# Hybrid encoder layer: `w_proj_b` as two block products of seven multiplications whose products take turns, with the b gates by way of DRAM and weight sums made in DRAM

## The chip, the cores and the metric

The kernel runs on one core of a Trainium2 chip. A core has five engines that each work through their own queue in order: TensorE (PE) multiplies matrices into PSUM, VectorE (DVE) and ScalarE (ACT) do elementwise work, GpSimd (POOL) does elementwise work in SBUF and issues DMAs, SyncE (SP) issues DMAs. Engines wait for each other through semaphores. The metric is the device time of one execution in microseconds. Everything is float32. A product of two matrices is made of three TensorE matmuls on float32r operands: each operand is split into a high part (`hi`, a cast) and a low part (`lo`, source minus high), and high x high, high x low and low x high are added up.

## The reference

One layer for 512 tokens of width 1024. What bears on the change is the mixer: one input projection feeds an S5 branch, a gated spatial branch and two gates, and the two branches are merged.

```python
n = rms_norm(h, mix_norm_g[i])
proj = n @ w_in[i]
xa = proj[..., :OFF_U]
zu = proj[..., OFF_U:OFF_V]
zv = proj[..., OFF_V:OFF_GA]
gate_a = jax.nn.sigmoid(proj[..., OFF_GA:OFF_GB])
gate_b = jax.nn.sigmoid(proj[..., OFF_GB:])
ya = s5_branch(xa, ...)
yb = sgu_branch(zu, zv, sgu_ln_g[i], sgu_ln_b[i], sgu_w[i], sgu_bias[i])
merged = gate_a * (ya @ w_proj_a[i]) + gate_b * (yb @ w_proj_b[i])
h = h + merged @ w_out[i]
h = h + memory_cross_attention(rms_norm(h, xattn_norm_g[i]), memn, w_q[i], w_k[i], w_v[i], w_xo[i])
h = h + swiglu(rms_norm(h, ffn_norm_g[i]), w_gate[i], w_up[i], w_down[i])
```

`yb` is 512 x 1024, `w_proj_b` 1024 x 1024. The S5 branch is two state-space scans over the sequence, a GELU and a gated projection (`w_glu`).

## The kernel before

**Weights.** All weights stream from DRAM by a plan: a list of entries, each with the loads to issue and the split to make. `next_w` (line 286) takes the next entry; it starts loads three entries ahead (`LOADS`), and makes high and low parts two entries ahead (`SPLITS`). Raw weights, high parts and low parts have three buffers each. Loads go through SP's queue.

**Two ways of multiplying.** `feat` (line 316) takes 256 output columns over all 512 tokens: a block of four 128-row tiles is 24 matmuls of 512 columns. `product` (line 1255) is one of the products of a two-by-two block multiplication in the Strassen-Winograd form: 24 matmuls of 256 columns. There a pair of 512 weight columns needs seven products instead of eight, with sums of quarters of the operands made beforehand. The feed-forward stage works so; `w_down`'s weight sums are made in DRAM by copies (`dsum`, SP) and accumulating copies (POOL), spread over the plan by `plan_sums` (line 216).

**The stages around the change.** After `zu` (the spatial branch, which yields `yb_hi`, `yb_lo` in slots E and D) a loop takes 256 columns at a time: gate b (`w_in`, 2 blocks of weights), whose sigmoid goes into `part` in slot A, then `w_proj_b` (2 blocks), whose result is multiplied into `part` (line 989). Four turns of the loop are 8 gate blocks and 8 `w_proj_b` blocks.

**S5 beside it.** S5 is a generator (`s5_program`) that `tick` advances between blocks. The scan over 64 chunks is 62 steps of four small VectorE instructions. Then come four octets of groups. For each octet `s5_outputs` (line 807) copies the shifted states `ss` (ScalarE, four copies) and multiplies into `py` on TensorE with `tt` (L822), `e` and `ss` (L823, L824); `emit` applies GELU and stores `y` to DRAM (`yd`) by eight small DMAs. `tt` holds the octet's kernels: made on TensorE (`pk`), stored to DRAM (`kd`) and loaded back by eight POOL DMAs (L743) into one buffer. Octets 2 and 3 have their `pk` between the outputs of the octets before. When all is drained (`finish_side`), `ygt` is loaded from `yd` (L1005) into memory that S5 has freed, split into `yg_hi` and `yg_lo`, and `w_glu` is multiplied.

**What sets the order.** The program is written in one order, and a scheduler with a model of times moves instructions of an engine against each other when the kernel is built. On the chip each engine then keeps that order.

Of the kernel before, what the change touches and what calls it, by code (L numbers as in the profile page):

```python
# [9 lines left out]
F32 = mybir.dt.float32  # L10
F32R = mybir.dt.float32r
# [6 lines left out]
P = 128  # L18
# [21 lines left out]
Q = 8  # L40
# [12 lines left out]
def hybrid_layer_kernel(  # L53
# [146 lines left out]

    DOWN, CHUNKS = (1, 5, 2, 6, 3, 7, 4), 6
    DSRC = {1: (0, 0), 2: (1, 0), 3: (1, 1)}
    dsum = {q: dp.tile([P, NF // 2, 512], F32, name=f"dsum{q}") for q in (4, 5, 6, 7)}
# [8 lines left out]
    def plan_sums(first, step):  # L216


        more = {5: lambda c: down_block(0, 1, c), 7: lambda c: down_block(1, 1, c),
                6: lambda c: down_sum(5, c), 4: lambda c: down_sum(6, c)}  # L220

        def start(q, i, jc, c):
            tc.keep_in_program_order(nc.sync.dma_start(down_sum(q, c), down_block(i, jc, c)))

        def add(q, c):
            nc.gpsimd.dma_start(down_sum(q, c), more[q](c), accum_op=ALU.add)

        j = first
        for q, i, jc in ((5, 0, 0), (7, 0, 1), (6, 1, 1), (4, 1, 0)):
            for c in range(CHUNKS):  # L230
                plan[j][1].append((0, lambda x=(q, i, jc, c): start(*x)))
                plan[j + step][1].append((0, lambda x=(q, c): add(*x)))
                j += step

    def plan_down(w, make_tokens, entries):
        for q in DOWN:
            for c in range(CHUNKS):
                got = {}

                def load(q=q, c=c, got=got):  # L240
                    src = down_block(*DSRC[q], c) if q in DSRC else down_sum(q, c)
# [10 lines left out]
    for c0 in range(0, SW, 256):  # L252
        plan_feat(w_in, c0, KD)
    plan_tok(w_in, OFF_V + 512, KD)
    first_copy = len(plan)
# [222 lines left out]
    def slot(tag, shape, dt, name):  # L478
        return sp.tile(list(shape), dt, tag=tag, name=name)

    def token_slot(name, shift=0):
# [44 lines left out]
    def s5_setup():  # L526
# [23 lines left out]
        for nm, src in (("br", s5_b_re), ("bi", s5_b_im), ("cr", s5_c_re), ("ci", s5_c_im)):  # L550
            if nm[0] == "b":
                row = s5p.tile([G, 2, 64, C], F32, tag="u", name="row" + nm)
                nc.sync.dma_start(row, src[0].rearrange("d g p c -> g d p c"))
                rows = row.rearrange("g d p c -> g (d p) c")
            else:
                row = s5p.tile([G, C, 2, 64], F32, tag="u", name="row" + nm)
                for d in range(2):
                    nc.sync.dma_start(row[:, :, d, :], src[0, d])
                rows = row.rearrange("g c d p -> g (d p) c")
            ps = aux("pbc", (P, C, G))  # L560
            for c in range(C):
                nc.tensor.transpose(ps[:, c, :], rows[:, :, c], ident[:G, :G])
            t = s5p.tile([P, G, C], F32, name="raw_" + nm)
            A_.copy(t, ps.rearrange("p c g -> p g c"))
            bc.append(t)
            yield 0.1
# [42 lines left out]
        st["pe"], st["pw"] = [], []  # L609
        for src in (pr, pi):  # L610
            pe = s5p.tile([P, G, Q], F32, name="pe%d" % len(st["pe"]))
            pw = s5p.tile([P, G, Q], F32, name="pw%d" % len(st["pw"]))
# [355 lines left out]
    yb_hi = slot("E", (P, KD, T), F32R, "yb_hi")  # L968
    yb_lo = slot("D", (P, KD, T), F32R, "yb_lo")
    yb = (yb_hi, yb_lo)  # L970

    def zu_evac(m, j, ps):
        h = m - OFF_U // P
# [6 lines left out]
        feat(w_in, c0, xn, KD, zu_evac)  # L980


    part = slot("A", (P, KD, T), F32, "part")

    def gb_evac(m, j, ps):
        nc.scalar.activation(part[:, m - OFF_GB // P, :], ps, AF.Sigmoid)

    def pb_evac(m, j, ps):
        nc.vector.tensor_tensor(part[:, m, :], ps, part[:, m, :], ALU.mult)

    for c0 in range(0, D, 256):
        feat(w_in, OFF_GB + c0, xn, KD, gb_evac)
        feat(w_proj_b, c0, yb, KD, pb_evac)
    finish_side()
    s5.close()
    mgx = ExitStack()
# [231 lines left out]
        nc.vector.tensor_tensor(pair[:, j, :], pair[:, j, :], ps, ALU.mult)  # L1228


    K0, K1, T0, T1 = slice(0, 4), slice(4, 8), slice(0, 256), slice(256, 512)
    a11, a12, a21, a22 = full[:, K0, T0], full[:, K1, T0], full[:, K0, T1], full[:, K1, T1]

    def make_op(q, i, src):
# [15 lines left out]
        make_op(3, 4, a12)  # L1250

    fn_q = lambda ks, ts: (fn_hi[:, ks, ts], fn_lo[:, ks, ts])
    ops = {1: fn_q(K0, T0), 2: fn_q(K1, T0), 7: fn_q(K0, T1), 4: fn_q(K1, T1)}

    def product(ps, u, q, start):

        hi, lo = next_w(u[0], u[1], q)
        for j in range(2):
            cs = slice(j * P, (j + 1) * P)
            for k in range(4):  # L1260
                a = (hi[:, k, cs], lo[:, k, cs])
                b = (ops[q][0][:, k, :], ops[q][1][:, k, :])
                for i, (x, y) in enumerate(((0, 0), (0, 1), (1, 0))):
                    nc.tensor.matmul(ps[:, j, :], a[x], b[y], start=start and j == k == i == 0,  # L1264
                                     stop=k == 3 and i == 2, skip_group_check=True)
        tick(2.7)

    def unit_bank(name):
        return bank(name).rearrange("p (j t) -> p j t", j=2)

    def unit_start(u):
        x, v = unit_bank("px"), unit_bank("pv")
# [84 lines left out]
    for i, u in enumerate(UNITS):  # L1357
# [7 lines left out]
        if i == 0:  # L1365
            split(*fn_q(K0, T1), s3)
        product(x, u, 6, False)
        u2 = stp[0].tile([P, 2, 256], F32, tag="u2", name="u2", bufs=2)
        u3 = np_.tile([P, 2, 256], F32, tag="ev", name="u3", bufs=2)
        nc.scalar.copy(u2, x)  # L1370
        if not final:
# [150 lines left out]
```

## Time and profile before

| what | value |
|---|---|
| three timed runs | 914.30, 914.52, 915.68 us (median 914.52) |
| the profiled execution | 915.85 us, its span 914.1 us |
| VectorE, ScalarE busy | 609.0 us, 458.7 us |
| DMA | 142.77 MB, mean 156 GB/s |
| gate b and `w_proj_b`, with three and a half S5 octets | 220 to 338 us of the span |
| the feed-forward units | 612 to 805 us |

The span runs from the first to the last recorded instruction; the execution's time holds a little more around it. In the views, "PE" is a matmul and "PEld" a weight load, a name such as `pf<-xn,whi` says what is written and read, and "<-" in brackets names what ended a wait. The chain of waits is followed back from the last instruction.

### The profile page before, as it was taken

Reading aid. Unit: us, or ns where it says so; the run is one execution under the profiler, and the core shown is the slowest. Engines: PE = TensorE matmul, PEld = TensorE weight load, DVE = VectorE, ACT = ScalarE, POOL = GpSimd, SP = SyncE. Lnnn points to the kernel's source line nnn. Section 1 sums busy time; section 2 is a strip of 40 time slices with the busy share of each in tenths; the row PEclk is TensorE's granted clock in tenths of the full one; section 3 lists DMA queues with packets and bytes.
Section 4 is the critical chain, followed back from the end, with each engine's and each line's share of the span. In section 5 each row is a group of like instructions: output and inputs, shape, how many; then the busy total and the mean of one; then the engine's idle time right before and its main releaser. Section 6 shows DMA issues by size and latency. Waiting matters only on the chain.

```text
span 914.1 us, 14130 instructions
## 1 busy us (share of the span) xinstructions
PE 897.4 (98%) x5510; PEld 789.2 (86%) x5510; DVE 609.0 (67%) x991; ACT 458.7 (50%) x671; POOL 109.1 (12%) x163
## 2 busy tenths in 40 slices
PE   7999999999999999999999999999999999999996
PEld 6888888888888887789998888999999999888875
DVE  5596662888753235868545444786778777899875
ACT  5542995244374333445434433655554555655663
POOL 3003210000025301502000001000000000000000
PEclk8999999999999999999999999999999999999999
DMA  8445263675546655686895217415456463246572
GB/s 269 127 120 151 85 164 126 181 205 133 141 138 158 144 185 156 216 260 191 244 291 147 71 68 233 113 65 142 119 154 144 118 160 94 70 147 207 188 241 82
DMA packets 105987, 142.77 MB, mean 156 GB/s; under 512 B 13232, under 2 KB 73152, under 8 KB 105920
## 3 DMA queue, kind: packets, MB, share of 16 engines
q1 hardware_dynamic: 90688, 120.14, 40.9%
q0 software_dynamic: 12064, 19.37, 12.9%
q10 hardware_dynamic: 3168, 2.36, 0.9%
q8 instruction: 43, 0.70, 0.3%
q14 instruction: 24, 0.20, 0.1%
HBM read 135.06 MB, written 29.85 MB: 180 GB/s over the span
## 4 chain that ended last, share of the span: by engine, by line
PE 86%; ACT 4%; DVE 4%; DMA 3%; issue 2%; POOL 1%; POOLq 0%; SPq 0%; ACTq 0%; DVEq 0%
PE pf L314 31%; PE pt L314 14%; PE px L1264 12%; PE pq L1264 6%; PE dx L314 5%; PE dq L314 3%; PE pv L1264 3%; PE dv L314 2%; PE pk L714 2%; DVE wlo L86 1%; PE ptr L466 1%; PE po L314 1%; PE psc L314 1%; DMA wraw<-dsum 1%; ACT whi L85 1%
## 5 line engine op out<-in xcount | busy, mean ns | idle before, releaser
L86 DVE TENSOR_TENSOR wlo<-wraw,whi 128x1024 fp32r<-128x1024 f32 (+1 forms) x130 | 157.9, 1216 | 130.5 <-ACT whi L85 128.0
L85 ACT CAST whi<-wraw 128x1024 fp32r<-128x1024 f32 x132 | 135.4, 1028 | 174.5 <-PE pf L314 79.7
L314 PE MATMUL pf<-xn,whi 128*128 128x512 f32 x448 | 140.5, 392 | 0.0
L314 PEld LDWEIGHTS pf<-xn,whi 128*128 128x128 f32 x448 | 83.7, 188 | 17.3 <-issue 0.2
L314 PE MATMUL pf<-xn,wlo 128*128 128x512 f32 x224 | 87.6, 391 | 0.0
L1264 PE MATMUL px<-fn,whi 128*128 128x256 f32 x480 | 83.8, 277 | 0.0
L1264 PEld LDWEIGHTS px<-fn,whi 128*128 128x128 f32 x480 | 72.6, 188 | 0.3 <-ACT u L1377 0.2
L85 ACT CAST whi<-b 128x1024 fp32r<-128x1024 f32 x40 | 42.1, 1054 | 55.0 <-PE px L1264 26.8
L86 DVE TENSOR_TENSOR wlo<-b,whi 128x1024 fp32r<-128x1024 f32 x40 | 48.9, 1223 | 28.5 <-ACT whi L85 28.5
L1264 PE MATMUL px<-fn,wlo 128*128 128x256 f32 x240 | 66.3, 276 | 0.0
L314 PE MATMUL dx<-whi,s 128*128 128x512 f32 x170 | 53.9, 391 | 1.4 <-ACT whi L85 1.0
L1264 PE MATMUL pq<-s,whi 128*128 128x256 f32 x320 | 55.0, 276 | 0.0
L314 PEld LDWEIGHTS pf<-xn,wlo 128*128 128x128 f32 x224 | 42.1, 188 | 8.5
L1264 PEld LDWEIGHTS pq<-s,whi 128*128 128x128 f32 x320 | 48.3, 188 | 0.2
L86 DVE TENSOR_TENSOR wlo<-t,whi 128x1024 fp32r<-128x1024 f32 x30 | 36.7, 1224 | 15.9 <-ACT whi L85 15.9
L85 ACT CAST whi<-t 128x1024 fp32r<-128x1024 f32 x30 | 31.6, 1053 | 31.0 <-PE pv L1264 11.3
L314 PE MATMUL pt<-whi,xn 128*128 128x512 f32 x128 | 43.4, 412 | 1.8 <-ACT xn L85 1.5
L1264 PEld LDWEIGHTS px<-fn,wlo 128*128 128x128 f32 x240 | 45.1, 188 | 0.0
L1264 PE MATMUL pq<-s,wlo 128*128 128x256 f32 x160 | 44.2, 276 | 0.0
L314 PE MATMUL pf<-hn,whi 128*128 128x512 f32 (+1 forms) x160 | 41.8, 349 | 0.0
L314 PEld LDWEIGHTS dx<-whi,s 128*128 128x128 f32 x170 | 31.7, 188 | 8.5 <-ACT whi L85 1.2
L314 PE MATMUL dx<-wlo,s 128*128 128x512 f32 x85 | 33.3, 391 | 0.7 <-DVE wlo L86 0.7
(380 smaller groups left out, 2175.3 us busy)
## 6 DMA issues: line engine op xcount, KB each, us to landing
wraw<-in_w_in_dram SPq DMA_DIRECT2D x36, 512.0 KB, 3.8
dsum<-in_w_down_dram SPq DMA_DIRECT2D x20, 512.0 KB, 5.3
wraw<-dsum SPq DMA_DIRECT2D x20, 512.0 KB, 3.6
b<-in_w_gate_dram SPq DMA_DIRECT2D x15, 512.0 KB, 3.6
b<-in_w_up_dram SPq DMA_DIRECT2D x15, 512.0 KB, 3.6
wraw<-in_w_down_dram SPq DMA_DIRECT2D x15, 512.0 KB, 4.1
dsum<-in_w_down_dram POOLq DMA_DIRECT2D x10, 512.0 KB, 7.3
dsum<-dsum POOLq DMA_DIRECT2D x10, 512.0 KB, 6.1
```

Of the source, the lines that this page charges most:

```text
L85: nc.scalar.copy(dst_hi, src)
L86: (lo_eng or nc.vector).tensor_tensor(dst_lo, src, dst_hi.bitcast(F32), ALU.subtract)
L314: nc.tensor.matmul(ps, a[x], b[y], start=start and i == 0, stop=stop and i == 2, skip_group_check=free)
L466: nc.tensor.transpose(ps[:, j, :], src[:, k * P:(k + 1) * P], ident)
L714: nc.tensor.matmul(ps[32 * j:32 * j + 32, q, :], bd[i][:, g].rearrange("p d c -> p (d c)"), lc(es[i], g), start=(i == 0), stop=False, tile ...
L1264: nc.tensor.matmul(ps[:, j, :], a[x], b[y], start=start and j == k == i == 0, stop=k == 3 and i == 2, skip_group_check=True)
```

## The change

`w_proj_b` becomes two block products, one for each half of its 1024 columns: 14 products in an order given by `PAIR`, in which the two halves take turns. For that

- the weight sums for products 4 to 7 are made in DRAM (`usum`): 8 copies on SP and 8 accumulating copies on POOL, and `plan_sums` now spreads these and `w_down`'s by planned time (75 us on, every 14; 200 us on, every 18);
- the operand sums of `yb`'s quarters (`sy`, `s4y`, and a quarter of `yb` overwritten) are made by 20 VectorE additions and 8 splits, beside gate b;
- the four gate b blocks come one after the other; their sigmoids go to DRAM (`gbd`) and come back into slot B, where `xn` was, once `xn` has been read; `part` moves there too;
- `yb_hi` and `yb_lo` begin 16 elements into their slots; some S5 tiles share buffers.

The core of the diff:

```diff
+    PAIR = ((0, 1), (0, 5), (0, 2), (0, 6), (1, 1), (0, 7), (1, 2), (1, 5), (1, 6), (0, 4), (1, 7), (0, 3), (1, 4), (1, 3))
+    MADE = (4, 5, 6, 7)
+    RAW = {1: (0, 0), 2: (1, 0), 3: (1, 1)}
...
+    def plan_pair(w):
+        kh = KD // 2
+        for i, q in PAIR:
+            if q in MADE:
+                if q not in usum:
+                    usum[q] = dp.tile([P, 2, kh, 256], F32, name=f"usum{q}")
+                src = usum[q][:, i]
+            else:
+                src = unit_block(w, i, *RAW[q])
...
+            plan.append(((w, i, q), [(LOADS, load)], lambda got=got: halves(got.pop("raw"))))
...
+        for q, r, c, more in ((5, 0, 0, (0, 1)), (7, 0, 1, (1, 1)), (6, 1, 1, 5), (4, 1, 0, 6)):
+            for n in range(dst(q, None)):
+                at(first, lambda x=(q, r, c, n): start(*x))
+                at(first + step, lambda x=(q, more, n): add(*x))
+                first += step
...
     for c0 in range(0, D, 256):
         plan_feat(w_in, OFF_GB + c0, KD)
-        plan_feat(w_proj_b, c0, KD)
+    plan_pair(w_proj_b)
...
-    plan_sums(first_copy + 2, 3)
+    plan_sums(lambda q, n: 2 if n is None else usum[q][:, n],
+              lambda r, c, n: unit_block(w_proj_b, n, r, c), 75, 14)
+    plan_sums(lambda q, n: CHUNKS if n is None else down_sum(q, n), down_block, 200, 18)
...
+    for i, fn_ in enumerate(quarter_sums(yb_hi, yb_lo, (sy[:, 0, 0], sy[:, 0, 1]), (sy[:, 1, 0], sy[:, 1, 1]),
+                                         s4y, sums)):
+        later(0.5 + 0.5 * i, fn_)
...
     def gb_evac(m, j, ps):
-        nc.scalar.activation(part[:, m - OFF_GB // P, :], ps, AF.Sigmoid)
-
-    def pb_evac(m, j, ps):
-        nc.vector.tensor_tensor(part[:, m, :], ps, part[:, m, :], ALU.mult)
+        z = np_.tile([P, T], F32, tag="ev", name="gbs", bufs=2)
+        nc.scalar.activation(z, ps, AF.Sigmoid)
+        nc.sync.dma_start(gbd[m - OFF_GB // P], z)
...
+    part, gbt = pg[:, 0], pg[:, 1]
+    for c in range(KD // 2):
+        nc.sync.dma_start(gbt[:, 2 * c:2 * c + 2], gbd[2 * c:2 * c + 2].rearrange("m p t -> p m t"))
+
+    def run_pair(w, put):
+
+        v, x, qb, u2, u3 = {}, {}, {}, {}, {}
+        for i, q in PAIR:
+            u = (w, i)
+            if q == 1:
+                v[i], x[i] = unit_bank("pv"), unit_bank("px")
+                product(x[i], u, 1, True)
+                nc.scalar.copy(v[i], x[i])
...
+            elif q == 6:
+                product(x[i], u, 6, False)
+                u2[i] = s5p.tile([P, 2, 256], F32, tag=("pw", "u2")[i], name="u2", bufs=1)
+                nc.scalar.copy(u2[i], x[i])
+            elif q == 7:
+                product(x[i], u, 7, False)
...
+    def put_part(i, f, ts, src):
+        m = slice(4 * i + 2 * f, 4 * i + 2 * f + 2)
+        V.tensor_tensor(part[:, m, ts], src, gbt[:, m, ts], ALU.mult)
+
+    run_pair(w_proj_b, put_part)
     finish_side()
```

How the change moves instructions on an engine shows in the built programs. On TensorE, before, this is where `py` of octet 3 begins (`pf_3068` is an output tile of the last `w_proj_b` columns; `u`, `tt`, `ss`, `e` are octet 3's operands):

```order
L314 MATMUL pf_3068<-yb_lo,whi 128x512
L314 MATMUL pf_3068<-yb_hi,wlo 128x512
L314 MATMUL pf_3068<-yb_hi,whi 128x512
L822 MATMUL py<-u,tt 128x64
L823 MATMUL py<-ss,e_2609 128x64
L824 MATMUL py<-ss,e_2614 128x64
```

Octet 3 stands in the middle of the last `w_proj_b` blocks; 41 of their matmuls are still to come behind it, and 63 matmuls (with `xn` and `yb`) lie between it and octet 2. After, on TensorE, this is where octet 2 ends (`e_2497`, `e_2502`) and octet 3 begins (`e_2662`, `e_2667`); all 14 products stand ahead of it:

```order
L864 MATMUL py<-ss,e_2502 128x64
L862 MATMUL py<-u,tt 128x64
L863 MATMUL py<-ss,e_2497 128x64
L864 MATMUL py<-ss,e_2502 128x64
L862 MATMUL py<-u,tt 128x64
L863 MATMUL py<-ss,e_2662 128x64
L864 MATMUL py<-ss,e_2667 128x64
```

Nothing is left between the two octets. And after, on TensorE, where octet 3 ends and `w_glu` begins (`pf` with `yg_hi`):

```order
L862 MATMUL py<-u,tt 128x64
L863 MATMUL py<-ss,e_2662 128x64
L864 MATMUL py<-ss,e_2667 128x64
L346 MATMUL pf_3411<-yg_hi,whi 128x512
L346 MATMUL pf_3412<-yg_hi,whi 128x512
L346 MATMUL pf_3455<-yg_hi,whi 128x512
```

The matmul behind octet 3 is now one that reads `yg_hi`, which comes from octet 3 itself. On ScalarE, before, behind the eight `ss` copies of octets 0 and 1, at the first `y`:

```order
L829 ACTIVATE y<-py 128x512
L816 COPY ss<-zh 64x8x63
L817 COPY ss<-zh 64x8x63
L816 COPY ss<-zh 64x8x63
L817 COPY ss<-zh 64x8x63
L832 DMA yd_241<-y 16x8x64 x4
L85 CAST whi<-wraw 128x1024 x2
```

After, on ScalarE, the same place (`u_2975` is the copy of the bank `px` that product (0,7) adds onto next):

```order
L85 CAST whi<-wraw 128x1024 x2
L869 ACT_TABLE_LOAD
L869 ACTIVATE y<-py 128x512
L856 COPY ss<-zh 64x8x63
L857 COPY ss<-zh 64x8x63
L856 COPY ss<-zh 64x8x63
L857 COPY ss<-zh 64x8x63
L872 DMA yd_245<-y 16x8x64 x4
L1121 COPY u_2975<-px 128x512
```

A copy on which TensorE waits now stands behind `y` and octet 2's `ss` copies, where before only weight casts did.

More of the change, by code (lines that the diff above doesn't have):

```diff
@@ L214, in down_sum, with plan_sums, at, start @@
         return dsum[q][:, 2 * c:min(2 * c + 2, NF // 2), :]
[L216 to L233, printed above, removed]
+    def plan_sums(dst, src, first, step):
+        ends = [0.0]
+        for key, _, _ in plan:
+            ends.append(ends[-1] + (5.4 if len(key) == 5 and key[0] is not w_k and key[0] is not w_v else 2.7))
+        def at(us, fn):
+            plan[next(j for j, e in enumerate(ends) if e >= us)][1].append((0, fn))
+        def start(q, r, c, n):
+            tc.keep_in_program_order(nc.sync.dma_start(dst(q, n), src(r, c, n)))
+        def add(q, more, n):
+            nc.gpsimd.dma_start(dst(q, n), src(*more, n) if isinstance(more, tuple) else dst(more, n),
+                                accum_op=ALU.add)
+        for q, r, c, more in ((5, 0, 0, (0, 1)), (7, 0, 1, (1, 1)), (6, 1, 1, 5), (4, 1, 0, 6)):
[3 more added lines that the diff above has]
+                first += step
     def plan_down(w, make_tokens, entries):
@@ L980, in hybrid_layer_kernel, with product @@
         feat(w_in, c0, xn, KD, zu_evac)
-    part = slot("A", (P, KD, T), F32, "part")
+    K0, K1, T0, T1 = slice(0, 4), slice(4, 8), slice(0, 256), slice(256, 512)
+    ops = {}
+    def product(ps, u, q, start):
+        hi, lo = next_w(u[0], u[1], q)
+        for j in range(2):
+            cs = slice(j * P, (j + 1) * P)
+            for k in range(4):
+                a = (hi[:, k, cs], lo[:, k, cs])
+                b = (ops[q][0][:, k, :], ops[q][1][:, k, :])
+                for i, (x, y) in enumerate(((0, 0), (0, 1), (1, 0))):
+                    nc.tensor.matmul(ps[:, j, :], a[x], b[y], start=start and j == k == i == 0,
+                                     stop=k == 3 and i == 2, skip_group_check=True)
+        tick(2.7)
@@ L985, in gb_evac @@
+    sy = slot("A", (P, 2, 2, 4, 256), F32R, "sy")
+    s4y = [np_.tile([P, 4, 256], F32R, tag="gain", name="s4y", bufs=2) for _ in range(2)]
+    sums = [s5p.tile([P, 2, 256], F32, tag=tag, name="sum", bufs=1) for tag in ("pw", "u2")]
+    for i, fn_ in enumerate(quarter_sums(yb_hi, yb_lo, (sy[:, 0, 0], sy[:, 0, 1]), (sy[:, 1, 0], sy[:, 1, 1]),
+                                         s4y, sums)):
+        later(0.5 + 0.5 * i, fn_)
+    gbd = dp.tile([KD, P, T], F32, name="gbd")
     def gb_evac(m, j, ps):
-        nc.scalar.activation(part[:, m - OFF_GB // P, :], ps, AF.Sigmoid)
@@ L1252, in hybrid_layer_kernel @@
     fn_q = lambda ks, ts: (fn_hi[:, ks, ts], fn_lo[:, ks, ts])
[L1253 to L1269, printed above, removed]
+    ops.clear()
+    ops.update({1: fn_q(K0, T0), 2: fn_q(K1, T0), 7: fn_q(K0, T1), 4: fn_q(K1, T1)})
     def unit_start(u):
```

82 lines of the change are left out of this document (70 added, 12 removed).

## The prediction

> **What bounds the kernel now.** I read the page first, then the table by stage, then the chain that ended last, and only then single instructions around the edited stage.
>
> ```profile
> span 914.1 us, 14130 instructions
> PE 897.4 (98%) x5510; PEld 789.2 (86%) x5510; DVE 609.0 (67%) x991; ACT 458.7 (50%) x671; POOL 109.1 (12%) x163
> ...
> PEclk8999999999999999999999999999999999999999
> ...
> PE 86%; ACT 4%; DVE 4%; DMA 3%; issue 2%; POOL 1%; POOLq 0%; SPq 0%; ACTq 0%; DVEq 0%
> ```
>
> TensorE is busy 98% of the span and owns 86% of the chain, at full clock nearly everywhere. No other engine is near that. So a matmul taken out is worth its own time, and a microsecond in which TensorE waits costs a microsecond: there is no slack in which it could be made up. The stages say the same, so I price everything on TensorE.
>
> ```profile
> core 0: us, PE busy (x) PEld busy (x) DVE busy (x) ACT busy (x) POOL busy (x), PEclk, DMA share, GB/s
> 226.00:346.00 120.00, 120.00 (x715) 102.50 (x714) 52.80 (x110) 53.80 (x61) 28.15 (x56) 1.00 0.57 155
> 346.00:390.00 44.00, 43.28 (x189) 33.98 (x188) 33.14 (x36) 19.67 (x30) 16.16 (x13) 1.00 0.60 178
> ...
> 425.00:585.00 160.00, 159.84 (x907) 139.65 (x906) 87.35 (x138) 70.25 (x126) 11.01 (x13) 1.00 0.62 177
> ...
> 615.00:790.00 175.00, 175.00 (x1545) 174.91 (x1544) 134.15 (x133) 92.64 (x112) 10.21 (x8) 1.00 0.50 127
> ```
>
> The edited stage (gate b, `w_proj_b`, and beside them the last S5 octets) is the first of these rows: TensorE has no gap, VectorE is under half busy, DMA at 0.57.
>
> **Term 1, the saved product: -5.5 us.**
>
> ```profile
> 176.91 77.13 PE pf L314 x340
> ...
> 612.87 2.72 PE pq L1264 x24
> ```
>
> 340 matmuls of 512 columns in 77.13 us are 0.2269 us each. `w_proj_b` is now 8 blocks of 24 of them: 192 x 0.2269 = 43.6 us. After, it is 14 products of 24 matmuls of 256 columns, and the feed-forward stage already runs that very product in 2.72 us: 14 x 2.72 = 38.1. Difference 5.5 us. I see no reason for another rate.
>
> **Terms 2 and 3, the S5 octets that lose their cover: +6.7 and +8.0 us.** Before, the last `w_proj_b` blocks stand on TensorE between S5's octet 2 and octet 3, and behind octet 3. After, all 14 products come first, then octet 2, octet 3 and the first `w_glu` matmul with nothing in between (the rows stand in the section on the change). Two latencies lose what hid them. First, `tt` has one buffer, so its load for octet 3 waits until octet 2's `py` has read it:
>
> ```profile
> 308.70 4.20 POOL L743 DMA_DIRECT2D tt<-kd  x8 [4.55 <-PE py L822]
> ...
> DMA to landing us min/median/max: 2.2/3.0/3.4
> ```
>
> Before, `py` released the same load, and its 4.2 us of issue and its landing lay under 14 us of `pf` matmuls. After, TensorE has nothing to do there. The eighth DMA starts 3.7 us after the release (8 of 0.53) and lands 3.0 later: 6.7 us; 5.9 to 7.1 with the shortest and longest landing.
>
> Second, from the last `py` matmul to the first operand of `w_glu`:
>
> ```profile
> 328.16 0.39 PE L824 MATMUL py<-ss,e 128*128 128x64 f32 x2
> ...
> 328.35 0.48 PE L314 MATMUL pf<-yb_lo,whi 128*128 128x512 f32 x1
> ...
> 328.58 0.60 ACT L829 ACTIVATE y<-py 128x512 f32<-128x512 f32 x1 [4.28 <-PE py L824]
> ...
> 329.20 1.77 SPq L832 DMA_DIRECT2D yd<-y  x4
> 332.79 1.77 SPq L1005 DMA_DIRECT2D ygt<-yd  x4
> ...
> 335.71 1.14 ACT L85 CAST yg_hi<-ygt 128x512 fp32r<-128x512 f32 x2 [2.35 <-DMA ygt<-yd]
> ...
> 336.42 1.29 DVE L86 TENSOR_TENSOR yg_lo<-ygt,yg_hi 128x512 fp32r<-128x512 f32 x2 [0.47 <-ACT yg_hi L85]
> ...
> 337.78 0.39 PE L314 MATMUL pf<-yg_hi,whi 128*128 128x512 f32 x1
> ...
> 340.49 0.68 DVE L86 TENSOR_TENSOR yg_lo<-ygt,yg_hi 128x512 fp32r<-128x512 f32 x1
> ```
>
> GELU, store, reload and cast: the first `yg_hi` is done at 335.71 + 0.62 = 336.33, that is 8.0 us behind 328.35. Before, TensorE filled all of it with `pf` matmuls and even came to `w_glu` late, at 337.78. After, nothing fills it. The last `yg_lo` ends 4.8 us after that first `yg_hi`, under the first 24 matmuls (5.4 us), so the later tiles add nothing. I keep 7.5 to 9 as bounds: the store's and the reload's landings are the uncertain part, and the queue ahead of them is a little different.
>
> **Term 4, ScalarE's queue in front of a product: +3.1 us.** Product (0,7) adds onto the bank which `u2` must first be copied from, and that copy now stands in ScalarE's queue behind twelve `ss` copies, a table load and a GELU. Their prices:
>
> ```profile
> 248.45 1.13 ACT L816 COPY ss<-zh 64x504 f32<-64x504 f32 x1
> ...
> 256.22 1.06 ACT L817 COPY ss<-zh 64x504 f32<-64x504 f32 x1
> ...
> 259.48 1.28 ACT L829 ACT_TABLE_LOAD   x1
> 260.77 0.60 ACT L829 ACTIVATE y<-py 128x512 f32<-128x512 f32 x1
> ...
> 308.85 14.39 PE pf L314 x63
> 328.55 17.80 PE pf L314 x78
> ...
> L1370 ACT COPY u<-px x10: 575/582/584, 619.2 to 790.6; 128x512 f32<-128x512 f32 x10
> ```
>
> Eight copies take 8.8 us (248.45 to 257.28). A `py` group takes 5.3 to 5.5 us (323.2 to 328.55). Count from the first product's start. ScalarE: a cast that waits for the first product, and the `pv` copy, end at 4.4; eight `ss` copies at 13.2; two casts at 15.2; table and GELU at 17.1; four `ss` copies at 21.6; the `u2` copy at 22.2. TensorE: `py` of octet 0 needs the fourth `ss` copy at 8.8 and could begin at 8.2 (0.6 lost), ends at 14.3; two more products end at 19.7; then (0,7) waits for 22.2, 2.5 lost. Bounds 0 (if these copies start earlier) and 6 (if the scan that feeds them ends 3 us later).
>
> **Term 5, the clock after such gaps: +5 us.**
>
> ```profile
> 12.00:16.00 4.00, 3.18 (x10) 2.04 (x9) 3.93 (x4) 3.25 (x7) 2.86 (x2) 0.62 0.80 242
> 16.00:18.00 2.00, 1.79 (x7) 1.63 (x8) 1.53 (x6) 0.77 (x3) 0.55 (x1) 0.50 0.84 257
> 18.00:20.00 2.00, 2.00 (x7) 1.57 (x6) 2.00 (x4) 2.00 (x5) 0.00 (x0) 0.55 0.79 208
> 20.00:22.00 2.00, 2.00 (x10) 1.66 (x9) 1.44 (x5) 0.22 (x3) 0.42 (x1) 1.00 0.93 270
> ```
>
> The only place of this trace where TensorE pauses for microseconds is the start, and right behind it the granted clock is 0.50. The lost clock is 0.38 x 4 + 0.5 x 2 + 0.45 x 2 = 3.4 us in one such episode. The change makes two gaps of 6.7 and 8.0 us. I take 2.5 us for each, since part of an episode falls on waiting; bounds 0 and 2 x 3.4. [...]
>
> **What costs nothing.** The operand sums are 20 additions and 8 low halves on VectorE and 8 casts on ScalarE. Nearest rows, and the scan that they share VectorE with:
>
> ```profile
> L86 DVE TENSOR_TENSOR wlo<-wraw,whi 128x1024 fp32r<-128x1024 f32 (+1 forms) x130 | 157.9, 1216 | 130.5 <-ACT whi L85 128.0
> ...
> L86 DVE TENSOR_TENSOR yb_lo<-zu,yb_hi x8: 684/692/693, 188.5 to 224.0; 128x512 fp32r<-128x512 f32 x8
> ...
> L801 DVE TENSOR_TENSOR zh<-sa,sb x62: 210/225/228, 161.1 to 247.2; 128x64 f32<-128x64 f32 x62
> ...
> wraw<-in_w_in_dram SPq DMA_DIRECT2D x36, 512.0 KB, 3.8
> ```
>
> 28 x 0.69 = 19.3 us of VectorE. Behind the last `yb_lo` (224.7), VectorE's new order holds 82 scan instructions, 25 of these 28 and 8 `wlo` until the scan's end: 82 x 0.22 + 25 x 0.69 + 8 x 1.22 = 45 us if none overlap, so the scan ends at 269 at the latest and not at 247; I take 268. Gate b begins at 176.91 + 192 x 0.2269 = 220.5 and its 192 matmuls end at 264.1; the first product is over at 266.8, so the late scan costs only what term 4 holds. The gates' trip (8 stores of 256 KB, 4 loads of 512 KB), 8 copies, 8 adds and six more weight loads lie beside TensorE: weights are loaded three entries ahead, 8.2 us of products, and such a load lands in 3.8. If that cover fails, one landing of about 4 us shows.
>
> The copies for `w_down` move later, into the feed-forward stage. There they meet the `t` accumulations on POOL's queue:
>
> ```profile
> L226 POOL DMA_DIRECT2D dsum<-dsum x12: 805/814/977, 189.9 to 519.1; - x12
> ...
> 628.46 1.30 POOL L164 DMA_DIRECT2D t<-in_w_gate_dram  x1 [39.09 <-DMA t<-in_w_gate_dram]
> ...
> 639.99 1.05 ACT L85 CAST whi<-t 128x1024 fp32r<-128x1024 f32 x1 [1.14 <-PE px L1264]
> ```
>
> 11.5 us between issue and use. The stage has a DMA share of 0.50, and the stage that carried these sums before ran TensorE dense at 0.62. I take 0; bounds -1 and 3.
>
> **Sum.** -5.5 + 6.7 + 8.0 + 3.1 + 5.0 = +17.3 us. The profiled execution took 915.85 (914.1 of span and 1.75 around it), so 933.2. It is 1.3 above the median of 914.52, so for timed runs I say **932**.
>
> **The rivals.**
> *The octets stay covered (faster).* If octets 2 and 3 did not stop TensorE, only terms 1 and 4 would remain: -5.5 + 3.1, or 912; without term 4, 909. It decides on one point: 15 us of matmuls must stand behind octet 2 or 3. Against it: TensorE's order has none. For it: only that both waits could turn out shorter than in the rows. 0.04.
> *The clock holds.* The gaps are there, but no half clock follows: 12.3 us more, 927. [...] Against it: the episode at the start came out of pauses under 1.5 us. 0.25.
> *The chains get longer.* The scan ends later than 268, so that `ss`, `py` of octet 0 and `u2` all slip (term 4 at 6), and the moved `w_down` sums delay a `t` (3): some 938. For it: VectorE's queue has little left between 226 and 268. 0.16.
> *The waits half open.* Only one of terms 2 and 3 shows and the clock holds: within 0.2%, some 915, or a little above. 0.03.
>
> **How the numbers follow.** My forecast (both waits, half clock behind each) has 0.52 and gives 932. Lower end of all terms: -5.5 + 5.9 + 7.5 + 0 + 0 - 1 = +6.9 (921); upper end -5.5 + 7.1 + 9 + 6 + 6.8 + 3 = +26.4 (941). The range 924 to 940 leaves out the covered and half-open cases and the tails. 0.2% (1.8 us) is about what a measurement of this kernel can tell from no change. Faster by more than that 0.05, within 0.02, slower 0.93.
>
> **What would show it.** Right: between the last `py` of octet 2 and the first of octet 3 TensorE idles for about 6.7 us, put down to `tt`; some 8 us between octet 3 and `yg_hi`; `PEclk` falls to 0.5 behind them; `u` copied from `px` ahead of a wait of about 2.5 us on (0,7); the products at 2.72 us each. Wrong: if `py` of octet 3 follows that of octet 2 directly, term 2 falls, with it most of the sum; if TensorE waits inside the products for `wlo` or `wraw`, I have missed a DMA; if the stages behind `w_glu` are longer than before, the moved sums cost.

## The result, and the profile after

| | before | changed |
|---|---|---|
| timed runs, median (range) | 916.12 us (914.30 to 923.35, 6 runs) | 951.64 us (949.17 to 958.41, 6 runs) |
| ratio to before, 95% interval | | 1.0378 [1.0327, 1.0429] |
| profiled execution, its span | 915.85, 914.1 us | 949.17, 947.4 us |

The change makes the kernel 3.8% slower. The direction was forecast, the size was not: 932 us with a range of 924 to 940. In the later rounds the kernel before itself lay between 914 and 927 us; so experiments are given as ratios to runs of the kernel before on the same chip, and single effects are read from stretches inside a profile.

The page of the changed kernel: span, busy times, slices, granted clock, and the chain's shares.

```profile
span 947.4 us, 14554 instructions
PE 901.9 (95%) x5654; PEld 801.6 (85%) x5654; DVE 634.2 (67%) x1029; ACT 466.8 (49%) x687; POOL 118.3 (12%) x171
...
PE   7999999999999957999999999699999999999996
...
PEclk9999999999998957999999999899999999999999
...
PE 79%; DMA 7%; ACT 5%; DVE 3%; issue 3%; POOL 2%; SPq 0%; ACTq 0%; POOLq 0%; DVEq 0%
```

TensorE's share of the chain fell from 86% to 79%, and DMA's rose from 3% to 7%. Counted from one, two dents show: slices 15 and 16 (332 to 379 us, S5 and `w_glu`; the clock fell already in slice 13), which were forecast, and slice 26 (592 to 616 us, the entry of the feed-forward stage), which was not. What TensorE waited for, by sum, number and longest, in the changed kernel:

```profile
PE py L862 <- DMA tt<-kd: 10.1, 1, 10.1
PE pf L346 <- ACT yg_hi L85: 7.8, 1, 7.8
PE ptr L498 <- DVE xs L490: 7.2, 1, 7.2
PE px L1034 <- ACT u L1121: 4.2, 1, 4.2
```

Three of the four are the forecast's terms 2, 3 and 4 (6.7, 8.0 and 3.1 there). The clock behind them, from the table by stretches of the changed kernel (busy time and count of each engine, granted clock, DMA share, GB/s):

```profile
286.00:291.00 5.00, 4.53 (x21) 4.53 (x22) 3.48 (x3) 2.89 (x4) 0.85 (x1) 0.51 0.60 166
...
332.00:344.00 12.00, 1.86 (x14) 1.76 (x14) 0.00 (x0) 0.60 (x1) 5.38 (x9) 0.64 1.02 270
344.00:354.00 10.00, 9.82 (x47) 9.63 (x46) 0.00 (x0) 0.14 (x1) 0.00 (x0) 0.50 0.18 32
354.00:361.00 7.00, 0.00 (x0) 0.00 (x0) 0.00 (x0) 0.53 (x2) 0.14 (x1) 0.50 0.48 115
361.00:366.00 5.00, 4.41 (x10) 3.48 (x11) 2.68 (x4) 3.62 (x5) 0.00 (x0) 0.50 0.93 338
...
611.00:616.00 5.00, 4.81 (x17) 4.09 (x18) 4.53 (x7) 3.19 (x5) 0.00 (x0) 0.59 0.49 93
```

Octet 3 (344 to 354) ran wholly at half clock and took 10.4 us instead of 5.4. The first `w_glu` matmuls lost 2.2 us (half of 4.41), product (0,7) lost 2.2 (0.49 x 4.53) and the feed-forward entry 2.0 (0.41 x 4.81).

Where the time is lost can be read from first starts. First the kernel before, then the changed one: the first `w_glu` matmul, the attention's first on `hn`, the feed-forward stage's first `pf` on `fn` (durations in ns, first and last start in us).

```profile
L314 PE MATMUL pf<-yg_hi,whi x16: 389/389/389, 337.8 to 348.0; 128*128 128x512 f32 x16
L314 PE MATMUL pf<-hn,whi x160: 278/389/477, 466.6 to 527.8; 128*128 128x512 f32 x96, 128*128 128x256 f32 x64
L314 PE MATMUL pf<-fn,whi x32: 388/392/397, 601.7 to 612.2; 128*128 128x512 f32 x32
```

```profile
L1034 PE MATMUL px<-yb_hi,whi x48: 278/280/583, 261.8 to 324.6; 128*128 128x256 f32 x48
L346 PE MATMUL pf<-yg_hi,whi x16: 389/394/796, 361.6 to 374.0; 128*128 128x512 f32 x16
L346 PE MATMUL pf<-hn,whi x160: 277/389/477, 491.9 to 553.0; 128*128 128x512 f32 x96, 128*128 128x256 f32 x64
L346 PE MATMUL pf<-fn,whi x32: 388/392/397, 636.2 to 646.7; 128*128 128x512 f32 x32
```

The delay is 23.8 us at `w_glu`, 25.3 at `hn` and 34.5 at `fn`. So some 24 us are lost in the S5 stretch, and 9.2 from `hn` to `fn` (144.3 us instead of 135.1). The first product began at 261.8, 2.3 us ahead of the 264.1 worked out: the start-up happened to be shorter, which is luck (the clock stood at 0.50 for 3.4 us there, from 11.0 to 14.4 us, and in the kernel before for 6.8, from 13.0 to 19.8; in run 1 the same product began at 265.0).

### The profile page after: what moved, and what is told of

It reads as the page before. It is cut to its first block, busy times and chain, and to the rows that moved or that the text cites. A ratio compares the mean times of both kernels' runs of the same rounds, so it can differ in the third digit from the quotient of the medians.

```text
span 947.4 us, 14554 instructions
## 1 busy us (share of the span) xinstructions
PE 901.9 (95%) x5654; PEld 801.6 (85%) x5654; DVE 634.2 (67%) x1029; ACT 466.8 (49%) x687; POOL 118.3 (12%) x171
## 4 chain that ended last, share of the span: by engine, by line
PE 79%; DMA 7%; ACT 5%; DVE 3%; issue 3%; POOL 2%; SPq 0%; ACTq 0%; POOLq 0%; DVEq 0%
PE pf L346 26%; PE px L1034 13%; PE pt L346 11%; PE pq L1034 6%; PE dx L346 6%; PE pv L1034 3%; PE dq L346 3%; DMA dsum<-in_w_down_dram 2%; PE dv L346 2%; DVE wlo L86 1%; PE ptr L498 1%; PE psc L346 1%; PE pk L754 1%; ACT whi L85 1%; DMA wraw<-in_w_in_dram 1%
## 5 line engine op out<-in xcount | busy, mean ns | idle before, releaser
L86 DVE TENSOR_TENSOR wlo<-wraw,whi 128x1024 fp32r<-128x1024 f32 (+1 forms) x136 | 165.0, 1216 | 104.3 <-ACT whi L85 103.6
L85 ACT CAST whi<-wraw 128x1024 fp32r<-128x1024 f32 x138 | 141.3, 1028 | 165.5 <-PE pf L346 67.2
L85 ACT CAST whi<-t 128x1024 fp32r<-128x1024 f32 x30 | 31.6, 1053 | 30.4 <-PE pv L1034 10.7
L257 POOL DMA_DIRECT2D dsum<-in_w_down_dram x12 | 13.4, 1121 | 164.4 <-DMA dsum<-in_w_down_dram 147.8
```

The costliest lines, as they stand in the source:

```text
L85: nc.scalar.copy(dst_hi, src)
L86: (lo_eng or nc.vector).tensor_tensor(dst_lo, src, dst_hi.bitcast(F32), ALU.subtract)
L257: nc.gpsimd.dma_start(dst(q, n), src(*more, n) if isinstance(more, tuple) else dst(more, n), accum_op=ALU.add)
```

## The experiments

The runs are numbered in the order in which they were made.

**The w_down sums at the feed-forward entry.** The third wait has its cause in four queues. In order of time, changed kernel:

```profile
591.65 1.43 SPq L254 DMA_DIRECT2D dsum<-in_w_down_dram  x1
...
602.85 1.05 ACT L85 CAST whi<-b 128x1024 fp32r<-128x1024 f32 x1 [11.10 <-DMA b<-in_w_gate_dram]
603.93 1.23 DVE L86 TENSOR_TENSOR wlo<-b,whi 128x1024 fp32r<-128x1024 f32 x1 [8.97 <-ACT whi L85]
605.07 0.68 DVE L1221 TENSOR_TENSOR h<-h,pt 128x512 f32<-128x512 f32 x1
...
606.80 0.15 DVE L476 TENSOR_SCALAR ms<-ms 128x1 f32<-128x1 f32 x1
...
608.85 0.90 POOL L257 DMA_DIRECT2D dsum<-dsum  x1 [10.39 <-DMA dsum<-in_w_down_dram]
609.44 0.91 POOL L477 TENSOR_TENSOR r<-ms,mhalf 128x1 f32<-128x1 f32 x1
610.38 1.41 DVE L490 SCALAR_TENSOR_TENSOR xs<-h,r,g_f 128x512 f32<-128x512 f32 x2 [3.43 <-POOL r L477]
...
611.19 1.11 PE L498 MATMUL ptr<-ident,xs 128*128 128x128 f32 x4 [7.17 <-DVE xs L490]
```

Read upwards: TensorE waits for `xs`, that for the rms factor `r` on POOL, and `r` stands behind an accumulating copy that waits for its plain copy, issued by SP at 591.65. Before that, the residual addition (`h`) stood on VectorE behind a `wlo` whose weights `b` landed late. `ms`, from which `r` is made, was done at 606.95 and `r` began at 609.44, so the copy held it for 2.5 us; the rest of the 7.2 comes from the late `h`.

```diff
-    plan_sums(..., down_block, 200, 18)
+    plan_sums(..., down_block, 240, 8)
```

Run 1:

> The changed kernel with the w_down sums planned from 240 us on, every 8 us, instead of from 200 on, every 18; they then end before the feed-forward stage. Theory POOL queue (the rms factor r of the feed-forward norm stands on POOL behind an accumulating DMA that waits for its copy): the 7.2 us wait of ptr for xs goes, and with it the half clock behind it, about 10 us in all: 939 to 942. Rival, the feed-forward stage's own loads fill the DMA engines and hold the norm whatever the sums do: still 948 to 952. If the sums' traffic also made the tt load of octet 3 land late (6.4 us against 3.0), that gap shrinks from 10.1 to about 7 and it is 936 to 939.

Measured: 1.0300 [1.0238, 1.0362], median 949.59. From `hn` to `fn` it took 137.7 us (496.2 to 633.9), and the wait for `xs` fell from 7.2 to 1.7. But a new wait of 3.0 us for `mt`, the memory norm, appeared: the same thing at another norm.

```profile
PE ptr L498 <- DVE mt L490: 3.0, 1, 3.0
...
PE ptr L498 <- DVE xs L490: 1.7, 1, 1.7
```

The mirror image, on the kernel before:

```diff
-    plan_sums(first_copy + 2, 3)
+    plan_sums(205, 18)    # by planned time, as in the changed kernel
```

Run 2:

> The kernel before with only the w_down sums moved: planned from 205 us on, every 18, as in the changed kernel, all else as before. Theory POOL queue: the same wait of several us appears between the w_xo products and the feed-forward stage, with a half clock behind it: 920 to 926. Rival, the wait needs the later S5 of the changed kernel, or the moved sums cost what was forecast (nothing): 914 to 917.

Measured: 1.0087 [1.0047, 1.0127]. The moved sums alone cost about 8 us. The stretch from `hn` to `fn` is 142.4 us instead of 135.1, with a wait for `xs` of 4.9:

```profile
PE ptr L469 <- DVE xs L461: 4.9, 1, 4.9
...
L317 PE MATMUL pf<-hn,whi x160: 278/389/477, 469.0 to 530.1; 128*128 128x512 f32 x96, 128*128 128x256 f32 x64
L317 PE MATMUL pf<-fn,whi x32: 388/392/397, 611.4 to 621.9; 128*128 128x512 f32 x32
```

To part queue from traffic, the accumulating copies were planned one step later:

```diff
+        lag = step if first == 75 else 2 * step
...
-                at(first + step, lambda x=(q, more, n): add(*x))
+                at(first + lag, lambda x=(q, more, n): add(*x))
```

Run 5:

> The changed kernel with each accumulating copy of the w_down sums planned two steps (36 us) behind its plain copy instead of one (18 us). Theory POOL queue: the copy has landed when POOL comes to the add, so POOL does not stand and the rms factor r behind it is on time: the stretch from the first matmul on hn to the first product on fn shrinks from 125.8 us to about 117 (before: 116.6), the wait of ptr for xs from 7.2 us to under 1, 941 to 943 in all, and no such wait appears in the memory norm. Rival, the feed-forward stage's own loads hold the norm: the stretch stays at 124 to 126.

1.0373 [1.0322, 1.0424], 144.1 us from `hn` to `fn`: nothing, but it tells nothing either. POOL's order had not changed, because the scheduler had moved the copies forward again. So they were also kept in program order:

```diff
-            nc.gpsimd.dma_start(...)
+            tc.keep_in_program_order(nc.gpsimd.dma_start(...))
```

Run 9:

> As the run with the adds two steps behind, where POOL's order had not changed since the scheduler had moved the adds forward again; now they are kept in the order of the program, so each stands on POOL one copy later than in the changed kernel. Theory POOL queue: the stretch from the first matmul on hn to the first product on fn shrinks from 125.8 us to 116 to 119, the wait of ptr for xs to under 1.5; 940 to 943 in all. Rival, the feed-forward stage's own loads hold the norm: the stretch stays at 123 to 126.

1.0373 [1.0330, 1.0417], 143.1 us. The wait of `r` for a copy was gone (here it waits for `ms`, line 477), the wait for `xs` fell to 2.7, and yet the stretch hardly shrank. The weights `b` still landed late (a 9.34 us wait of their cast), and waits for `fn` (2.0) and a weight cast (2.9) took the place. Queue and traffic are two locks on one door. Then both at once, by having the sums done earlier:

```diff
-    plan_sums(..., down_block, 200, 18)
+    plan_sums(..., down_block, 90, 14)
```

Run 13:

> The changed kernel with the w_down sums planned from 90 us on, every 14, so that the last of them stands on POOL ahead of the first t of the feed-forward stage and SP's last copy ahead of that stage's loads. Theory (moved sums cost at the entry of the feed-forward stage, by POOL's queue and by their traffic): from the first matmul on hn to the first pf on fn 144.3 us becomes 135 to 138 (before: 135.1), 941 to 944 in all. Rival, the new plan moves the wait to another norm or into the S5 stretch: 947 or more.

1.0274 [1.0212, 1.0336], median 945.36. The stretch is 136.8 us, nearly that of before, and the wait for `xs` is 0.4:

```profile
L346 PE MATMUL pf<-hn,whi x160: 278/389/477, 492.2 to 553.4; 128*128 128x512 f32 x96, 128*128 128x256 f32 x64
L346 PE MATMUL pf<-fn,whi x32: 388/392/398, 629.0 to 639.5; 128*128 128x512 f32 x32
```

With the mirror image this settles that loss: the moved sums added 7.3 us to this stretch in the kernel before, and doing them early took 7.5 out of it here.

**The clock.** Matmuls that nobody reads, put into the two gaps:

```diff
             later(1, lambda: emit(ps))
+            warm = aux("warm") if o > 1 else None
+            for _ in range({2: 42, 3: 32}.get(o, 0)):
+                tc.keep_in_program_order(nc.tensor.matmul(warm, yb_hi[:, 0, 0:P], yb_hi[:, 0, :],
+                                                          start=True, stop=True))
```

Run 4:

> The changed kernel with 42 matmuls of 512 columns that nothing reads between octets 2 and 3, and 32 behind octet 3; the result is unchanged. Theory, half the clock is a cost of its own: both waits stay as long as they are (10.1 and 7.8 us), but py of octet 3 takes 5.4 us instead of 10.4, and the first w_glu matmuls run at full clock: 5 + 2 us less, 944 to 946. Rival, the slow octet 3 comes from somewhere else (late operands, contention): 951 to 953, and the granted clock stays at 0.5.

1.0287 [1.0222, 1.0353], median 950.52. The stretches of this run:

```profile
336.00:346.00 10.00, 9.97 (x46) 7.95 (x44) 0.00 (x0) 0.60 (x1) 5.37 (x9) 1.00 1.03 278
346.00:352.00 6.00, 5.82 (x50) 5.81 (x51) 0.00 (x0) 0.24 (x1) 0.00 (x0) 1.00 0.42 76
...
359.00:362.00 3.00, 0.60 (x3) 0.48 (x3) 0.56 (x1) 1.14 (x2) 0.00 (x0) 1.00 0.97 281
362.00:366.00 4.00, 4.00 (x12) 3.14 (x11) 2.08 (x4) 2.52 (x3) 0.00 (x0) 0.57 0.99 355
```

Octet 3 (346 to 352) now ran at full clock in 5.5 us, 5 less, as expected. The way to `yg_hi` took 2 us longer this time, so a pause of 2.4 us was left behind the fillers, and behind it the clock was 0.57 (362 to 366). From the first product to `w_glu` it took 96.7 us instead of 99.8: 3 less, where octet 3 alone was to give 5. That half clock is a cost of its own is shown; the total does not show it clearly.

**Term 4: who holds ScalarE.** Its fourth `y` store was issued 2.3 us late, so all eight went to SP:

```diff
-                (nc.sync, nc.scalar)[l % 2].dma_start(ydo[l], y[C * l:C * l + C])
+                nc.sync.dma_start(ydo[l], y[C * l:C * l + C])
```

Run 3:

> The changed kernel with all eight y stores of an octet issued by SP, none by ScalarE. Theory: the 4.2 us wait of product (0,7) for u2 comes from ScalarE, held 2.3 us at issuing its fourth y store while the DMA queues are full, so the wait and the half clock behind it go: 4 to 6 us less, 944 to 947. Rival, the forecast's own account (the late scan and twelve ss copies in ScalarE's queue): about 2 us of wait stay, 948 to 950. Rival, SP is held in place of ScalarE and weight loads come late: 951 or more.

1.0372 [1.0306, 1.0437]. The wait for `u` fell from 4.2 to 2.5 us, and those for `tt` and `yg_hi` rose to 11.0 and 9.4: the stores only changed the queue that they hold up. The forecast's account (3.1) stands with a share for the stores.

**One tt.** `tt` gets a second place; in runs 7 and 8 octets 2 and 3 also stand ahead of the last three products, and run 8 has run 5's edit besides:

```diff
-            tt = s5p.tile([P, GO, P], F32, tag="tt", name="tt")
+            tt = s5p.tile([P, GO, P], F32, tag=("tt", "etmp")[o % 2], name="tt")
...
+        for o in (0, 2):    # outputs 0, 1, then kernels 2, 3, then outputs 2, 3
```

Run 6:

> The changed kernel with tt in two places (odd octets in the place of etmp), so octet 1 and octet 3 need not wait until the octet before has been multiplied; kernels 2 and 3 are made behind both of the first octets. TensorE's order still has octets 2 and 3 behind all 14 products. Theory single tt: the 10.1 us wait between octets 2 and 3 goes and octet 3 runs at full clock; only the 8 us wait for yg_hi and the half clock behind it stay: from the first product to the first w_glu matmul 83 to 87 us instead of 99.8, 934 to 938 in all. Rival, another operand of octet 3 (e, ss) or the later load of tt takes the place of the wait: 94 us or more.

Run 7:

> As the run before, and TensorE's order has octets 2 and 3 ahead of the last three products, which are then 8.2 us of cover for the way from octet 3 to yg_hi; same instructions otherwise. Theory cover: 14 products (38.1), four octets (21.6), two pk (7.8) and the wait for u2 (4 to 6 with its half clock) remain: 71 to 76 us from the first product to the first w_glu matmul, 921 to 927 in all, most of what is left being the feed-forward wait. Rival, octets 2 and 3 are not ready so early and the waits move ahead of the last products: 80 us or more.

Run 8:

> The run before with the adds two steps behind as well. Theory: the two repairs add up, since their waits lie in different stages: 910 to 917, the saved 5.5 us of the product against what is left of the wait for u2, so at most 0.5% from the kernel before, on either side. Rival, something else of the change costs (usum, gate stores and loads, later scan): 922 or more.

None of the three was faster than the changed kernel (1.0378 [1.0327, 1.0429]): 1.0469 [1.0413, 1.0525], 1.0438 [1.0372, 1.0503] and 1.0436 [1.0393, 1.0480]. In the profiles of the first and the third, `w_glu` began at 368.0 and 364.2 us instead of 361.6. The wait for `tt` stayed at 12.6 and 10.9 us, now because octet 3's kernel came late in its own chain (its `ks` could only be made and stored at 326). And octets 0 and 1, now back to back, brought something new, in the first of these runs:

```profile
269.00:272.00 3.00, 2.05 (x20) 1.95 (x18) 0.00 (x0) 2.95 (x4) 0.00 (x0) 1.00 1.03 401
272.00:274.00 2.00, 2.00 (x18) 2.00 (x17) 0.00 (x0) 1.96 (x3) 0.00 (x0) 0.84 0.93 298
274.00:288.00 14.00, 14.00 (x67) 14.00 (x67) 5.87 (x6) 9.61 (x11) 1.81 (x7) 0.50 0.78 201
```

After a pause of only 0.95 us the clock fell to half in the middle of dense `py` matmuls and stayed there for 14 us. That was no fixed price: in the third of these runs the same two octets, behind a pause of 0.94 us, ran at full clock to their end.

```profile
268.00:271.00 3.00, 2.06 (x19) 1.95 (x19) 0.00 (x0) 2.96 (x3) 0.00 (x0) 1.00 1.04 413
271.00:274.00 3.00, 3.00 (x29) 3.00 (x29) 0.00 (x0) 2.94 (x5) 1.16 (x1) 1.00 0.74 238
274.00:286.00 12.00, 12.00 (x107) 12.00 (x106) 9.77 (x9) 11.10 (x11) 0.85 (x8) 1.00 0.83 196
```

So the rival of the first run held, and "single `tt`" was too narrow a theory.

**The late scan.** In the changed kernel the scan ends at 265.0 us and not at 247.4, since VectorE does 28 instructions for `yb`'s quarters at the same time. First they were put on GpSimd (run 11 adds run 9's edit, and puts octet 3 ahead of the last three products):

```diff
-            nc.vector.tensor_tensor(temps[i], f(x), f(y), op)
+            nc.gpsimd.tensor_tensor(temps[i], f(x), f(y), op)
```

Run 10:

> The changed kernel with the 20 additions for yb's quarters on GpSimd instead of VectorE (1.3 to 2 us each there instead of 0.69). The order that follows on TensorE has 14 us of products between octets 2 and 3, octet 3 still behind all products. Theory late scan: the 28 VectorE instructions put the scan's end from 247 to 265 us and with it every octet; now it ends before 252, the wait of octet 3 for tt goes, and only the way from octet 3 to yg_hi (8 us and a half clock) is left: from the first product to the first w_glu matmul 78 to 86 us instead of 99.8, 932 to 940 in all. Rival, the octets are paced by their own chain (one buffer for ks and y, POOL's queue with the additions in it), not by the scan: 92 us or more, 945 or more.

Run 11:

> Both runs before together, and octet 3 ahead of the last three products. Theory: the late scan, the way from octet 3 to yg_hi without cover and the adds on POOL are all there is: from the first product to the first w_glu matmul 68 to 76 us, hn to fn 116 to 119, 914 to 924 in all. Rival: octet 3 is not ready 8 us ahead of the end of the products, and its wait moves ahead of them: 80 us or more in the first stretch.

1.0489 [1.0443, 1.0535] and 1.0610 [1.0567, 1.0653]. The scan was no earlier (269.7): with the additions on GpSimd, scan instructions of 0.22 us took up to 1.33 (0.23 at most in the changed kernel), and the scan's 248 instructions together 73.0 us instead of 55.0.

```profile
L841 DVE TENSOR_TENSOR zh<-sa,sb x62: 212/225/1326, 161.5 to 269.5; 128x64 f32<-128x64 f32 x62
...
L1051 POOL TENSOR_TENSOR sum<-sum,yb_lo x12: 1263/1292/2267, 215.2 to 260.4; 128x512 f32<-128x512 f32 x12
```

Inconclusive for the theory. So the sums were left out altogether, alone and with the early `w_down` sums:

```diff
-    for i, fn_ in enumerate(quarter_sums(yb_hi, yb_lo, ..., s4y, sums)):
-        later(0.5 + 0.5 * i, fn_)
+    quarter_sums(yb_hi, yb_lo, ..., s4y, sums)
+    ops.update({5: ops[1], 6: ops[2], 3: ops[4]})
```

Run 12:

> The changed kernel without the sums of yb's quarters: 20 additions, 8 casts and 8 low halves are left out, and products 3, 5, 6 and 7 take plain quarters; all 14 products, usum and the gates' trip stay. TensorE's order then has 8 products between octets 2 and 3 and 2 behind octet 3. Theory late scan: the scan ends at 246 to 250 us as before and not at 265, the wait of octet 3 for tt goes, that for yg_hi shrinks to under 4; from the first product to the first w_glu matmul 99.8 becomes 50 to 62 us, since two octets then run under gate b, and the time 908 to 922 with the feed-forward wait still in it. Rival, one tt and the single ks and y buffer pace the octets whatever the scan does: waits of 15 us or more stay in that stretch, 935 or more.

Run 14:

> Both edits together: without the sums of yb's quarters (products 3, 5, 6 and 7 take plain quarters), and the w_down sums early. Theory: the late scan and the w_down sums at the feed-forward entry are all that the change loses; what is left is the saved product: 906 to 914, faster than before by up to 1%. Rival, another part (usum, the gates by DRAM) costs too: 918 or more.

1.0231 [1.0179, 1.0284], median 941.84, and 1.0106 [1.0069, 1.0143], median 929.32. The scan ended at 245.6 and `w_glu` began at 352.2, in the second run at 347.9. So leaving the sums out is worth 9.4 of the 23.8 us at `w_glu`. That is the late scan together with what goes with it, 28 instructions less on VectorE, 8 less on ScalarE and another order on TensorE; the scan's share alone is not shown. Both expectations were missed, by 20 and 15 us, and the times are in the ranges of the rivals: with the scan on time and the sums out of the way the kernel is still slower than before. In the first of these runs, behind octet 3:

```profile
337.75 1.77 SPq L872 DMA_DIRECT2D yd<-y  x4
346.21 0.39 SPq L124 DMA_DIRECT2D wraw<-in_w_proj_a_dram  x1
347.20 1.77 SPq L1151 DMA_DIRECT2D ygt<-yd  x4
```

`ygt` was issued 7.7 us behind the `y` stores, where before it was 1.8 (331.0 to 332.8). A weight load stands ahead of it on SP, which waits 6.5 us until a split (`wlo`) lets a raw buffer go, and the splits wait for the last products. The cover of the last octet now holds up its own way out.

**Could the saved product be had at all?** The kernel before, with the same 5.45 us taken from TensorE and nothing else: 24 matmuls of `w_proj_b` left out.

```diff
-        for i, (x, y) in enumerate(((0, 0), (0, 1), (1, 0))):
+        for i, (x, y) in enumerate(((0, 0), (0, 1), (1, 0))[:2 if two else 3]):
...
+                    kk == 0 and fresh, kk == nk - 1, not fresh, w is w_proj_b and (j, k) in ((0, 1), (0, 2), (1, 1)))
```

Run 15:

> The kernel before with 24 matmuls of w_proj_b left out, three of each block's 24 (low part by high part, on three of eight tiles), so TensorE has 5.45 us less to do there, as in the change, and nothing else is touched. TensorE's order now has 9 w_proj_b matmuls behind octet 3 instead of 41. Theory S5 bound: w_glu cannot start before yg_hi, 7.8 us behind octet 3, and TensorE already came only 1.5 us later than that; the saved work turns into a wait of 4 to 7 us for yg_hi with a half clock behind it, and the ratio to the kernel before is 0.998 to 1.004. Rival, TensorE's saved work counts in full: w_glu starts at 332 us instead of 338 without such a wait, ratio 0.992 to 0.995.

0.9996 [0.9962, 1.0030]. The work that went came back as a wait:

```profile
PE pf L314 <- ACT yg_hi L85: 5.6, 1, 5.6
...
L314 PE MATMUL pf<-yg_hi,whi x16: 389/389/796, 336.5 to 348.2; 128*128 128x512 f32 x16
```

`w_glu` began at 336.5 instead of 337.8, after a wait of 5.6 us and with a clock of 0.57 behind it (336 to 340): the last of these matmuls starts at 348.2, before at 348.0. S5's way to `yg_hi` was a second bound 1.5 us behind TensorE, and no saving of TensorE time in this stretch counts beyond that unless S5 is faster too.

## Why the prediction was wrong, step by step

| step | forecast | measured in the profile |
|---|---|---|
| 1 saved product | -5.5 | about -4: a product took 2.83 here (0.118 us a matmul), not 2.72 |
| 2 `tt` between octets 2 and 3 | 6.7 | 10.1 |
| 3 octet 3 to `yg_hi` | 8.0 | 7.8 |
| 4 ScalarE ahead of product (0,7) | 3.1 | 4.2 |
| 5 half clock | 5.0 | 9.4 = 2.2 + 5.0 + 2.2 |
| moved `w_down` sums | 0 (-1 to 3) | 9.2 = 7.2 + 2.0 |
| start-up; remainder | 0 | -2.3; -1.1 |
| sum | +17.3 | +33.3 |

- **The step that failed is the last cost of nothing.** "There they meet the `t` accumulations on POOL's queue", and then "I take 0; bounds -1 and 3": I looked at `t` and not at what else stands on POOL there, the rms factors of a norm for which TensorE has no cover, nor at the burst of loads that this stage begins with. More than half of the miss of 16 us lies here; runs 2 and 13 show it from both sides.
- **Term 2** had the right mechanism and the issue time; the landing was mis-sized. Its eight loads landed after 6.6 us and not 3.0. Median landings in the stretch behind octet 2, before and changed:

```profile
tt<-kd POOLq DMA_DIRECT2D x8, 64.0 KB, 3.0
```

```profile
wraw<-in_w_proj_a_dram SPq DMA_DIRECT2D x1, 512.0 KB, 11.5
tt<-kd POOLq DMA_DIRECT2D x8, 64.0 KB, 6.6
dsum<-in_w_down_dram POOLq DMA_DIRECT2D x1, 512.0 KB, 6.0
```

  And in run 9:

```profile
tt<-kd POOLq DMA_DIRECT2D x8, 64.0 KB, 3.3
```

  TensorE stands still, but SP does not: weight loads and sums run ahead and fill the DMA engines (share 1.02 from 332 to 344). The sums are not needed for that: in run 13 none was issued between 318.1 and 342.6, and behind three weight loads issued from 332.5 on the `tt` loads still landed after 6.0 us. In run 9 the last weight load ahead of them was issued at 328.8; they landed after 3.3 us though the share was 0.92 (332 to 339.2), and octet 3 followed octet 2 after 6.6 us (332.6 to 339.2): the forecast's figure. What decides between 3 and 6 us is not shown further than that.
- **Term 3** was right to 0.2 us. **Term 4** was right in kind; I had not counted that a held store adds to it.
- **Term 5**: I took 2.5 us for each gap. Octet 3, behind the first of them, spent its whole 10.4 us at 0.50 and lost 5.0. It had no gap among its 64-column matmuls, and the clock did not come back in that time; in `w_glu` it was back 4.4 us behind the first 512-column matmul (361.6 to 366.0). Shorter pauses were followed by a lower clock too: 2.4 us in run 4 by 0.57, 0.95 in run 6 by 0.50. In the changed kernel's trace the stretches of half clock that end inside the span lasted 3.41 us at the start, 6.83 at product (0,7), 30.72 from behind octet 2 into `w_glu` and 6.83 at the feed-forward entry, in the trace of before 6.83 at the start: each a multiple of 3.41, and why is not shown.
- **The premise** "a microsecond in which TensorE waits costs a microsecond" held; its other half, "a matmul taken out is worth its own time", fell in run 15. The rows for it stood in the prediction: first `yg_hi` ready at 336.33, `w_glu` at 337.78. I read them as the price of a lost cover and not as the limit of the gain.
- **The rivals.** "The chains get longer" had the right direction (938) and named the sums and the scan, at a third of their price. The late scan was taken to cost only what term 4 holds; run 12 shows 9.4 us for it and for the work that goes with it. These 9.4 us do not come on top of the table: they lie in its waits and half clock (the wait for `tt` is 3.2 us in run 12).

Open: why, with the scan on time, `w_glu` still starts 10 to 14 us late. The waits are in the profiles (in run 14: 5.3 for `yg_hi`, 5.4 in three waits for copies of `px`, and behind the wait for `yg_hi` four `w_glu` matmuls took 2.08 us, before 1.07; in run 12 also SP's queue, above), but no run takes them away one at a time. No version here beats the kernel before, and run 15 bounds what less TensorE work gains in this stretch while S5 stays as it is: 0.4% at most.

## What to carry to other kernels

Before pricing a saving on the busiest engine, look for the next chain that ends at the same place: here it was ready 1.5 us before it was needed, so a saving of 5.5 us could give at most that. Work that was moved off the path still stands in some queue: list what stands behind each moved wait at its new place, above all small operations such as a norm's factor. And once TensorE stopped here, transfers ran ahead and the very landing for which it waited took 6.6 us instead of 3.0, while octet 3's short matmuls then ran 10.4 us at 0.50: the gap cost more than the wait.

## What the runs showed of the hardware

- Two octets back to back are 96 matmuls of 64 columns, 10.7 us at the 0.111 us of one at full clock. In run 6, behind a pause of 0.95 us, the clock was 0.84 from 272 to 274 and 0.50 for the 14 us that followed, although TensorE was busy throughout; in run 8, behind a pause of 0.94 us, they kept 1.00. So neither the pause nor the short matmuls decide alone, and what does is open. In the changed kernel octet 3's 48 matmuls of 64 columns began at 0.50 and were still at 0.50 when they ended 10.4 us later.
- The stretches of half clock that end inside the span lasted 6.83 us in the trace of before and 3.41, 6.83, 30.72 and 6.83 us in that of the changed kernel.
- Two-input additions of 128x512 float32 took 1.29 us on GpSimd (run 10) against 0.69 on VectorE (changed kernel). VectorE's scan instructions of 0.22 us took up to 1.33 in run 10 and 0.23 at most in the changed kernel.
- In the changed kernel 24 matmuls of 256 columns took 2.83 us on `yb`'s operands; in the kernel before, 24 of the feed-forward stage's took 2.72.
